# Hybrid encoder layer on one core: the first half's second norm through ones matmuls, its output projection ahead of the second half's mixers, the sample's modulation loads in one buffer

## The chip, the core and the metric

The kernel runs on one core of a Trainium2 chip. The core has TensorE (PE in the rows; PEld is its weight load), VectorE (DVE), ScalarE (ACT), GpSimd (POOL) and SyncE (SP), each with a queue that it works off in order, and 16 DMA engines. Times are device microseconds (us) of one execution; the metric is the median of three runs.

## What is computed

One layer of a streaming encoder over two groups of frames that share the weights: a prompt of 1024 frames and a sample of 64, of 1024 channels each. Around the code that the change touches, the reference is:

```python
mod = (silu(c) @ w_ada + b_ada).reshape(B, 6, 1, D_MODEL)     # one set for the prompt, one for the sample
h = rms_norm(x, norm_mix) * (1 + scale1) + shift1
u = h @ w_in                                                  # split into conv, delta, pool, attention
mix = concat([conv, gated_delta, pool, stick_breaking]) @ w_out
x = x + gate1 * mix
h2 = rms_norm(x, norm_ffn) * (1 + scale2) + shift2            # the second norm
x = x + gate2 * ((silu(h2 @ w_gate) * (h2 @ w_up)) @ w_down)
```

`rms_norm` is `x * rsqrt(mean(x * x) + eps) * g` over the 1024 channels. The gated delta mixer solves a lower triangular system in each chunk of 64 frames and carries a state from chunk to chunk.

## The kernel before

Channels lie on the 128 partitions, eight tiles deep, and frames along the free dimension. The frames are worked in two halves: HA, the first 512 of the prompt, and HB, the other 512 and the 64 of the sample (576 columns). Every large product is made of three passes, weight-high by x-high, weight-high by x-low and weight-low by x-high: `load_w` loads a weight tile (wraw, 512 KB, from SyncE's queue), ScalarE copies its high part (whi) and VectorE subtracts for the low part (wlo), each with two buffers. `gemm_fm` then runs the matmuls into a bank that `gemm_bank` gives. Up to the sixth pair of the FFN's tiles that is one of two banks; from there (`wide`) it takes turns over eight, some of which the delta mixer and the attention also use, by a counter `turn` that every call moves on.

The order of the code at the end of the kernel is: projection and mixers of HA (`mixers`: `delta`, `sb_attn`, and for HA `conv` and `pool`), projection of HB, mixers of HB with the sample's attention, output projection and second norm of HA (`out_proj`), FFN of HA (`ffn`, which calls `conv` and `pool` of HB on its way), then `out_proj` and `ffn` of HB. A scheduler lays the instructions out per engine by that order as priority, by what is ready, and with `tc.high_priority()` for what others wait for; so on each engine HA's FFN and HB's mixers interleave. An engine then keeps to its list.

- The delta mixer solves its systems in blocks. VectorE writes nl, SyncE sends it to memory (nld), GpSimd brings it back transposed, does the substitution of the smallest blocks (fst, fsu) and writes X; `pw<-cst,X` on TensorE is the first matmul that needs it. HB has three such blocks, the third with the sample.
- The second norm of a half: after each output tile m, `residual` adds it to x (xA in HA, VectorE), `sumsq` squares it (sq, ScalarE) and adds it to acc (VectorE). Then `rstd_of` sums acc over the partitions by a product with a matrix of ones (pn, in fp32, two instructions of TensorE), and ScalarE takes Ln and Exp. `modulate` writes nrm (VectorE), its high part hi (ScalarE) and its low part lo (VectorE), from which the FFN's first pg starts.
- The modulation of the sample: `ada_sample` loads 32 tiles wads of 512 KB with SyncE, behind a weight's load in its queue, and VectorE multiplies and sums each. Their buffers are the tiles k2 and q2 of the attention. They are shared out over the tiles of HA's FFN from tile t0_s on. The prompt's loads are named wadt. The tile raw holds the delta mixer's inputs, and at the end parts of HB's mixed output.

## Time and profile before

| | us |
|---|---|
| median of three runs | 1483.85 |
| lowest, highest | 1481.14, 1489.55 |
| the profiled execution | 1479.19 |
| its span | 1477.4 |
| TensorE busy in it | 1396.9 |
| VectorE busy | 1025.3 |
| ScalarE busy | 662.5 |

The span is the time between the first and the last instruction; all times of rows count from its start. The mean clock granted to TensorE over the span is 0.976 of full speed, where 1.00 stands for 2.4 GHz and 0.5 for 1.2 GHz. In a timeline row a number in brackets is the idle time just before the instruction, with what ended it; several instructions in one row are marked xN. Ends of matmuls are modelled, so the starts of neighbours tell better what one takes.

### The profile page before, as it was taken

What the parts mean: (1) busy time and instruction counts of PE and PEld (TensorE: products, weight loads), DVE (VectorE), ACT (ScalarE), POOL (GpSimd) and SP (SyncE); (2) the same over time, 40 slices, a digit from 0 to 9 for tenths busy, and PEclk for the clock granted to TensorE, in tenths of its full rate; (3) what the DMA queues carried; (4) which work ended last, traced back from release to release, by engine and by line L of the source; (5) the groups of instructions that cost most, each with busy time, mean ns of one, the idle gap of its engine ahead of it and who ended that gap; (6) DMA issues with size and microseconds to landing.
All of it is one profiled execution on the core that took longest, in us unless ns stands there. A gap on an engine that the chain in (4) does not pass through costs nothing.

```text
span 1477.4 us, 24764 instructions
## 1 busy us (share of the span) xinstructions
PE 1396.9 (95%) x9824; PEld 1219.4 (83%) x9824; DVE 1025.3 (69%) x1816; ACT 662.5 (45%) x1191; POOL 119.8 (8%) x246
## 2 busy tenths in 40 slices
PE   8999999979997799799999899999899999999998
PEld 5777898868875477587877688889799999999998
DVE  8788997954898998846766677764755455554444
ACT  4467555744664478447766332222522222222221
POOL 0005000500014000500140000000000000000000
PEclk9999999989998799999999999999999999999999
DMA  8776655555845223424324566542322222222222
GB/s 319 246 221 183 194 169 177 172 166 164 266 141 160 70 90 96 124 76 134 111 75 133 164 226 209 196 140 86 127 77 84 86 86 86 77 82 86 87 86 93
DMA packets 98547, 205.43 MB, mean 139 GB/s; under 512 B 30848, under 2 KB 40928, under 8 KB 98432
## 3 DMA queue, kind: packets, MB, share of 16 engines
q1 hardware_dynamic: 89888, 191.68, 38.8%
q0 software_dynamic: 8544, 12.17, 3.8%
q8 instruction: 77, 1.26, 0.3%
q14 instruction: 38, 0.31, 0.1%
HBM read 175.57 MB, written 28.24 MB: 138 GB/s over the span
## 4 chain that ended last, share of the span: by engine, by line
PE 73%; DVE 14%; DMA 6%; ACT 3%; issue 3%; SPq 0%; POOL 0%; DVEq 0%; ACTq 0%
PE pg L138 61%; DVE cy L126 2%; DMA wadt<-in_wadat_dram 2%; PE psC L141 2%; PE pk L138 2%; DVE wlo L123 2%; DMA X<-xd 1%; PE psO L141 1%; PE z L141 1%; DVE dnf L126 1%; PE pw L138 1%; DVE wadt L212 1%; DVE lo L126 1%; ACT whi L117 1%; DVE xA L126 1%
## 5 line engine op out<-in xcount | busy, mean ns | idle before, releaser
L138 PE MATMUL pg<-hi,whi 128*128 128x288 f32 (+1 forms) x1504 | 503.7, 336 | 9.9 <-DVE sbo L123 2.7
L138 PE MATMUL pg<-hi,wlo 128*128 128x288 f32 (+1 forms) x1504 | 498.7, 332 | 3.4 <-DVE wlo L123 3.4
L138 PE MATMUL pg<-lo,whi 128*128 128x288 f32 (+1 forms) x1504 | 498.0, 331 | 1.6 <-DVE lo L126 1.6
L117 ACT ACTIVATE whi<-wraw 128x1024 fp32r<-128x1024 f32 (+2 forms) x192 | 199.7, 1041 | 474.0 <-PE pg L138 414.4
L138 PEld LDWEIGHTS pg<-hi,whi 128*128 128x128 f32 x1504 | 285.4, 190 | 41.4 <-issue 9.2
L138 PEld LDWEIGHTS pg<-hi,wlo 128*128 128x128 f32 x1504 | 285.1, 190 | 28.3 <-DVE wlo L123 4.7
L138 PEld LDWEIGHTS pg<-lo,whi 128*128 128x128 f32 x1504 | 285.7, 190 | 25.5 <-issue 2.1
L123 DVE TENSOR_TENSOR wlo<-wraw,whi 128x1024 fp32r<-128x1024 f32 (+2 forms) x192 | 230.4, 1201 | 106.2 <-ACT whi L117 103.5
L138 PE MATMUL pg<-g,whi 128*128 128x288 f32 (+1 forms) x1056 | 251.4, 330 | 4.1 <-DVE xA L126 1.9
L138 PEld LDWEIGHTS pg<-g,whi 128*128 128x128 f32 x1056 | 177.5, 188 | 20.2 <-DVE xA L126 3.2
L138 PE MATMUL pg<-g,wlo 128*128 128x288 f32 (+1 forms) x528 | 171.4, 328 | 0.0
L126 DVE SCALAR_TENSOR_TENSOR xs<-pg,mod,xs 128x288 f32<-128x288 f32 (+2 forms) x288 | 106.4, 412 | 85.8 <-PE pg L138 84.6
L123 DVE TENSOR_TENSOR fa<-fa,pg 128x288 f32<-128x288 f32 (+1 forms) x66 | 35.0, 531 | 101.5 <-PE pg L138 98.3
L138 PEld LDWEIGHTS pg<-g,wlo 128*128 128x128 f32 x528 | 99.2, 188 | 7.5
L126 DVE SCALAR_TENSOR_TENSOR cy<-cvb,vec,cy 128x512 f32<-128x512 f32 (+1 forms) x120 | 93.4, 792 | 0.2
L126 DVE SCALAR_TENSOR_TENSOR xA<-pg,mod,xA 128x512 f32<-128x512 f32 x96 | 69.6, 745 | 13.0 <-PE pg L138 12.6
L114 ACT ACTIVATE e<-e 128x512 f32<-128x512 f32 (+4 forms) x100 | 52.1, 521 | 0.9
L138 PE MATMUL pg<-mixs,whi 128*128 128x288 f32 x256 | 50.8, 295 | 0.0
L212 DVE CUSTOM_DVE_ANT_0 wadt<-wadt,cb,vec 128x1024 f32<-128x1024 f32 x32 | 40.9, 1280 | 12.2 <-DMA wadt<-in_wadat_dram 12.1
L114 ACT ACTIVATE zs<-zs 128x512 f32<-128x512 f32 (+4 forms) x50 | 25.8, 516 | 45.8 <-DVE zs L123 43.6
L212 DVE CUSTOM_DVE_ANT_0 wads<-wads,cb,vec 128x1024 f32<-128x1024 f32 x32 | 41.0, 1280 | 5.1 <-DMA wads<-in_wadat_dram 5.0
L138 PEld LDWEIGHTS pg<-mixs,whi 128*128 128x128 f32 x256 | 41.0, 188 | 0.1
(299 smaller groups left out, 1842.3 us busy)
## 6 DMA issues: line engine op xcount, KB each, us to landing
wraw<-in_wgate_dram SPq DMA_DIRECT2D x44, 512.0 KB, 3.2
wraw<-in_wup_dram SPq DMA_DIRECT2D x44, 512.0 KB, 3.3
wraw<-in_wdown_dram SPq DMA_DIRECT2D x44, 512.0 KB, 3.2
wadt<-in_wadat_dram SPq DMA_DIRECT2D x32, 512.0 KB, 4.7
wads<-in_wadat_dram SPq DMA_DIRECT2D x32, 512.0 KB, 4.4
wraw<-in_wfm_dram SPq DMA_DIRECT2D x30, 512.0 KB, 3.7
wraw<-in_wout_dram SPq DMA_DIRECT2D x16, 512.0 KB, 3.5
xA<-in_xa_dram SPq DMA_DIRECT2D x16, 256.0 KB, 5.4
```

Source lines behind the costliest of these rows:

```text
L114: nc.scalar.activation(out, in_, func, bias=bias, scale=scale)
L117: nc.scalar.activation(out, in_, ACTF.Copy)
L123: nc.vector.tensor_tensor(out=out, in0=a, in1=b, op=op)
L126: nc.vector.scalar_tensor_tensor(out, a, s, b, op0, op1)
L138: return nc.tensor.matmul(out, lhsT=lhsT, rhs=rhs, start=start, stop=stop)
L141: nc.tensor.matmul(out, lhsT=lhsT, rhs=rhs, start=start, stop=stop, skip_group_check=True)
L212: nc.vector.tensor_tensor_reduce(out=junk, in0=w, in1=cbt[g], scale=1.0, scalar=V("b_ada", col), op0=ALU.mult, op1=ALU.add, accum_out=mod[ ...
```

## The change

HA's second norm no longer adds squares on VectorE: each m's squares go to TensorE as they come, as one of eight products with the matrix of ones that accumulate in one bank, taken from the pool "cv" and not by `gemm_bank`. HB's second norm stays. `rstd_of` and `modulate` take the finished sum. The tiles wads lie in the delta mixer's raw tile, of which there is one, and start at tile 8 of the FFN in place of 12. The call of HA's output projection and the last loads of the prompt's modulation stand ahead of HB's mixers.

```diff
--- before.py
+++ after.py
@@ -252,7 +252,7 @@
 
     def ada_sample(j0, j1):
         for j in range(j0, j1):
-            t = sb.tile([P, 1024], F32, tag=("k2", "q2")[j % 2], name="wads")
+            t = dn.tile([P, 1560], F32, tag="raw", name="wads")[:, 0:1024]
             with behind():
                 nc.sync.dma_start(out=t, in_=io["wadat"][j])
             ada_dve(t, 16 + j, (1,))
@@ -264,9 +264,9 @@
         tt(s2[:, :, g], s2[:, :, g], V("norm_ffn"), ALU.mult)
 
 
-    def rstd_of(h, acc, early):
-        pns = []
-        for c0, n in h.chunks:
+    def rstd_of(h, acc, early, summed=None):
+        pns = [] if summed is None else [(summed, 0, h.n)]
+        for c0, n in h.chunks if summed is None else []:
             pn = (PD if pns else PC)("pn") if early else gemm_bank("pn")
             mm(pn[:, 0:n], C("ones"), acc[:, c0:c0 + n])
             pns.append((pn, c0, n))
@@ -305,8 +305,8 @@
             act_(h.hi[k][:, c], t[:, c], ACTF.Identity, bias=sh)
             stt(h.lo[k][:, c], t[:, c], sh, f(h.hi[k][:, c]), ALU.add, ALU.subtract)
 
-    def modulate(h, acc, sc, shift0, in_place=False):
-        r = rstd_of(h, acc, in_place)
+    def modulate(h, acc, sc, shift0, in_place=False, summed=None):
+        r = rstd_of(h, acc, in_place, summed)
         h.hi, h.lo = [], []
         for k in range(KT):
             modulate_k(h, k, r, sc, shift0, in_place)
@@ -1049,14 +1049,20 @@
                 split(h, t, hi[k], lo[k])
             load_x(h, h.samp)
         acc = new_acc()
+        pn = None if h.samp else PC("pn")
         for m in range(KT):
             for ps, c0, n in gemm_fm(h, io["wout"][m], hi, lo, order):
                 with tc.high_priority():
                     residual(h, m, 16, ps, c0, n)
             with tc.high_priority():
-                sumsq(h, acc, m)
+                if h.samp:
+                    sumsq(h, acc, m)
+                else:
+                    q = ST("sq")
+                    act_(q[:, 0:h.n], h.xt[m][:, 0:h.n], ACTF.Square)
+                    mm(pn[:, 0:h.n], C("ones"), q[:, 0:h.n], m == 0, m == KT - 1)
         with tc.high_priority():
-            modulate(h, acc, s2, 24)
+            modulate(h, acc, s2, 24, summed=pn)
 
     def ffn(h):
         if h.samp and DEFER:
@@ -1103,7 +1109,7 @@
                 if c == FT // FCH - 1:
                     nc.sync.dma_start(out=h.y[:, m], in_=h.xt[m][:, 0:n_])
 
-        t0_s = 12
+        t0_s = 8
         a = gate(0)
         for c in range(FT // FCH):
             if not h.samp and c == 1:
@@ -1178,11 +1184,11 @@
     while len(ada_left) > 8:
         ada_step()
     scale2(0)
-    mixers(HB)
     out_proj(HA)
     with tc.high_priority():
         while ada_left:
             ada_step()
+    mixers(HB)
     ffn(HA)
     out_proj(HB)
     ffn(HB)
```

What the scheduler makes of it shows in three places. The numbers in names (pw_4582) count buffers and differ between the two programs.

On TensorE, in HB's second delta block near 490 us, before:

```order
L141 MATMUL z<-q_5591,k_5589 128x512 x2
L138 MATMUL py<-W,X 64x64 x16
L138 MATMUL px<-X,W 64x64 x16
L141 MATMUL psC<-sh,omu_r 128x512
L141 MATMUL psC<-sl,omu_r 128x512
L141 MATMUL psO<-ph,v_5590 128x512
L141 MATMUL psC<-sh,u_r 128x512
L138 MATMUL pw<-Y,nl 64x64 x16
L141 MATMUL psO<-pl,v_5590 128x512
L138 MATMUL pn<-acc,cst 128x512
L141 MATMUL psC<-sl,u_r 128x512
```

and with the change:

```order
L138 MATMUL pw<-Y,nl 64x64 x5
L141 MATMUL psC<-sl,u_r 128x512
L141 MATMUL z<-q_6011,k_6009 128x512 x2
L138 MATMUL pn<-sq,cst 128x512
L138 MATMUL py<-W,X 64x64 x13
L138 MATMUL pn<-sq,cst 128x512
L138 MATMUL py<-W,X 64x64 x3
L138 MATMUL px<-X,W 64x64 x16
L141 MATMUL psC<-sh,omu_r 128x512
L141 MATMUL psC<-sl,omu_r 128x512
```

Here py and px belong to the triangular solve and psC, psO and z to the attention. The norm's sum is complete ahead of the last py of a solving step, where one pn of acc stood behind the next step's pw. Six more pn<-sq stand further up, five of them ahead of the block's first pw<-cst,X.

On TensorE, ahead of the first matmul of HB's third delta block (near 627 us in the trace of before), before:

```order
L138 MATMUL pg<-g_7466,whi 128x512 x2
L138 MATMUL pg<-g_7466,wlo 128x512
L138 MATMUL pg<-g_7541,whi 128x512 x2
L138 MATMUL pg<-g_7541,wlo 128x512
L138 MATMUL pw_5063<-cst,X 64x64
L141 MATMUL psO<-pl,v_5815 128x512
L141 MATMUL psC<-sl,u_r 128x128
L138 MATMUL pw_5063<-cst,X 64x64 x15
L141 MATMUL z<-q_6041,k_6039 128x384 x2
```

and with the change:

```order
L138 MATMUL pg<-hi_4703,whi 128x512
L138 MATMUL pg<-lo_4704,whi 128x512
L138 MATMUL pg<-hi_4703,wlo 128x512
L138 MATMUL pg<-hi_4709,whi 128x512
L141 MATMUL psO<-pl,v_6460 128x128
L138 MATMUL pw_5483<-cst,X 64x64
L138 MATMUL pg<-lo_4710,whi 128x512
L138 MATMUL pg<-hi_4709,wlo 128x512
L138 MATMUL pg<-hi_4715,whi 128x512
L138 MATMUL pw_5483<-cst,X 64x64 x15
```

pg<-g is the second product of the FFN's pair of tiles, pg<-hi the first of the next tile. The first pw<-cst,X of the block stood behind the last pg<-g; now it stands in the next tile's products, with 31 instructions more between it and the second block's.

On SyncE's queue, where HA's FFN loads its weights and HB's last delta block begins, before:

```order
L323 DMA wraw<-in_wdown_dram 128x1024 x2
L865 DMA out_dn_p_dram<-S_p 128x128
L323 DMA wraw<-in_wup_dram 128x1024
L323 DMA wraw<-in_wgate_dram 128x1024
L853 DMA mixB<-kbe 128x2x256
L626 DMA gate<-udnB 128x2x64
L491 DMA mixB<-sbo 64x512
L176 DMA xs<-in_xb_dram 128x576
L323 DMA wraw<-in_wup_dram 128x1024
L777 DMA nld_124<-nl 64x128 x2
```

and with the change:

```order
L323 DMA wraw<-in_wdown_dram 128x1024 x2
L257 DMA wads<-in_wadat_dram 128x1024 x2
L865 DMA out_dn_p_dram<-S_p 128x128
L323 DMA wraw<-in_wup_dram 128x1024
L491 DMA mixB<-sbo 64x512
L323 DMA wraw<-in_wgate_dram 128x1024
L257 DMA wads<-in_wadat_dram 128x1024
L853 DMA mixB<-kbe 128x2x256
L626 DMA gate<-udnB 128x2x64
L257 DMA wads<-in_wadat_dram 128x1024
L323 DMA wraw<-in_wup_dram 128x1024
L176 DMA xs<-in_xb_dram 128x576
```

Four loads wads now stand among these weights, each behind the one before in the only buffer; in the program before the first stands 14 rows further down than the last row here.

## Rows read from the trace of the kernel before

**Rows 1.** The page: busy time by engine, and the chain that ended last.
```profile
PE 1396.9 (95%) x9824; PEld 1219.4 (83%) x9824; DVE 1025.3 (69%) x1816; ACT 662.5 (45%) x1191; POOL 119.8 (8%) x246
...
PE 73%; DVE 14%; DMA 6%; ACT 3%; issue 3%; SPq 0%; POOL 0%; DVEq 0%; ACTq 0%
...
L117 ACT ACTIVATE whi<-wraw 128x1024 fp32r<-128x1024 f32 (+2 forms) x192 | 199.7, 1041 | 474.0 <-PE pg L138 414.4
```

**Rows 2.** Stretches of 40 us: busy time and instructions by engine, clock, DMA.
```profile
core 0: us, PE busy (x) PEld busy (x) DVE busy (x) ACT busy (x) POOL busy (x), PEclk, DMA share, GB/s
440.00:480.00 40.00, 30.18 (x226) 23.34 (x225) 35.65 (x57) 18.56 (x31) 19.46 (x37) 0.87 0.50 152
480.00:520.00 40.00, 29.15 (x224) 20.68 (x220) 39.23 (x62) 17.73 (x37) 0.66 (x2) 0.79 0.25 66
520.00:560.00 40.00, 38.75 (x260) 30.54 (x260) 38.43 (x63) 29.91 (x57) 1.09 (x2) 1.00 0.30 94
560.00:600.00 40.00, 40.00 (x303) 31.07 (x301) 36.27 (x64) 29.87 (x52) 4.25 (x8) 1.00 0.45 126
600.00:640.00 40.00, 29.57 (x168) 21.77 (x168) 27.64 (x53) 19.44 (x47) 18.68 (x39) 0.91 0.30 94
800.00:840.00 40.00, 33.22 (x143) 24.74 (x142) 27.04 (x44) 16.67 (x31) 0.00 (x0) 0.91 0.50 160
840.00:880.00 40.00, 40.00 (x176) 32.70 (x175) 28.82 (x39) 16.37 (x21) 0.00 (x0) 1.00 0.59 208
```

**Rows 3.** Timeline of TensorE: start, us, engine, line, operation, idle before.
```profile
397.03 1.03 PE L138 MATMUL pl<-dne,cst 128*128 128x512 f32 x2
...
466.52 0.44 PE L138 MATMUL pw<-cst,X 64*64 64x64 f32 x2 [8.60 <-DMA X<-xd]
...
486.30 0.80 PE L141 MATMUL psO<-pl,v 128*128 128x512 f32 x1 [1.26 <-DVE pl L123]
486.90 2.07 PE L138 MATMUL pn<-acc,cst 128*128 128x512 f32 x2
```

**Rows 4.** Timeline of VectorE from the last xA of HA to nrm.
```profile
477.43 0.75 DVE L126 SCALAR_TENSOR_TENSOR xA<-pg,mod,xA 128x512 f32<-128x512 f32 x1 [1.28 <-PE pg L138]
...
486.16 0.68 DVE L123 TENSOR_TENSOR acc<-acc,sq 128x512 f32<-128x512 f32 x1
...
495.47 2.73 DVE L126 SCALAR_TENSOR_TENSOR nrm<-xA,s,acc 128x512 f32<-128x512 f32 x4
```

**Rows 5.** Timelines of VectorE and TensorE around the third block.
```profile
587.39 0.68 DVE L126 SCALAR_TENSOR_TENSOR nl<-pkk,W 128x512 f32<-128x512 f32 x1
...
627.11 0.44 PE L138 MATMUL pw<-cst,X 64*64 64x64 f32 x2 [6.06 <-DMA X<-xd]
...
632.17 0.39 PE L138 MATMUL pg<-hi,whi 128*128 128x512 f32 x1
632.40 0.40 PE L138 MATMUL pg<-lo,whi 128*128 128x512 f32 x1
```

**Rows 6.** The instructions that write or read wads, and the page on wlo.
```profile
L257 SPq DMA_DIRECT2D wads<-in_wadat_dram x32: 327/328/526, 808.3 to 965.5; - x32
L212 DVE CUSTOM_DVE_ANT_0 wads<-wads,cb,vec x32: 1273/1280/1289, 812.1 to 970.1; 128x1024 f32<-128x1024 f32 x32
  DMA wads<-in_wadat_dram: 5.0, 9
...
DMA to landing us min/median/max: 3.4/4.4/6.5
...
L123 DVE TENSOR_TENSOR wlo<-wraw,whi 128x1024 fp32r<-128x1024 f32 (+2 forms) x192 | 230.4, 1201 | 106.2 <-ACT whi L117 103.5
```

**Rows 7.** Timelines of VectorE and TensorE near the end of the sample's attention.
```profile
826.38 1.22 DVE L123 TENSOR_TENSOR wlo<-wraw,whi 128x1024 fp32r<-128x1024 f32 x1
...
827.66 0.79 PE L138 MATMUL pg<-hi,wlo 128*128 128x512 f32 x1 [2.03 <-DVE wlo L123]
...
838.17 0.47 PE L138 MATMUL pg<-hi,whi 128*128 128x512 f32 x1 [2.65 <-DVE sbo L123]
```

## The prediction

> **What bounds the kernel now.** I read the page first: TensorE is busy 95% of the span and VectorE 69%, and the chain that ended last is 73% TensorE [rows 1]. An average over stages hides where the other 5% lies, so the second view is the table by stretches of 40 us [rows 2]. It shows three kinds of stretch. From 440 to 520 VectorE is nearly full (35.65 and 39.23 of 40) while TensorE is busy 30.18 and 29.15 and its granted clock is 0.87 and 0.79: here HA's output projection, its second norm, its first FFN matmuls and HB's delta mixer meet, and VectorE decides. From 600 to 640 both have holes. From 640 on TensorE is nearly full, as 840 to 880 shows, except for 800 to 840 (33.22, clock 0.91). So a microsecond of VectorE is worth something only before 640, and a microsecond of TensorE work after that is worth a microsecond.
>
> The third view, the timeline around the long waits, names what ends them. TensorE sits 8.60 us before HB's second delta block and 6.06 us before the third, both for the DMA X<-xd [rows 3, 5]. The second wait follows a chain that nothing shortens: VectorE writes nl at 587.39, SyncE sends it, GpSimd transposes, substitutes and sends X, and TensorE starts at 627.11 [rows 5]: 39.7 us from nl to the matmul. HA's second norm begins when the last residual xA ends at about 478.1, its sum goes to TensorE as pn at 486.90, and the first nrm, from which the FFN starts, is written at 495.47 [rows 3, 4].
>
> **The change, part by part.**
>
> *Squares on TensorE.* Seven additions acc<-acc,sq go, about 0.6 us of VectorE each (0.68 with the tail that overlaps the next) [rows 4], 4.2 us in all. Four of them lie before the 8.60 us wait, whose chain started ahead of the first of them, so these give nothing there. The last three, 1.8 us, lie where VectorE decides. On TensorE one pn of two instructions goes and eight come. Such a matmul took 1.03 us at the full clock (pl<-dne) and 2.07 us at the half clock (pn) [rows 3], so eight cost 8.2 us and the net is about +7.2. In the new order five of the eight stand ahead of the matmul that waits 8.60 us: 5.2 us, hidden by that wait. One follows it and two stand among the py, where TensorE waits for VectorE anyhow: the wait of 1.26 us in [rows 3] is one of this stretch. I cost all eight at nothing; without that cover they would cost up to 7.2.
>
> *The order.* With HA's projection ahead of HB's mixers in the code, the instructions up to about 424 us stay where they were, and after that HA's norm and FFN stand ahead of pieces of HB's mixers. On VectorE 10.0 us of work then stand between the start of the last xA (477.43) and the first nrm, which so comes at about 487.4 in place of 495.47, and the FFN starts some 7 us sooner. That alone is no gain: the wait at 627 follows nl, and nl must be early for it. In the new order, with the durations of the rows of before, VectorE has 2.1 us more to do up to nl than it had. Its idle time from 440 to 600 is 4.35, 0.77, 1.57 and 3.73 us [rows 2], 10.4 in all, so nl moves between +2.1 (no idle filled) and -8.3 (all filled). Most of that idle time is for matmuls and DMAs that stay, so I take a value near the upper end, **-2.0**, and keep both. On SyncE's queue nl's two DMAs now stand behind the loads of two weights and a write of mixB that they stood ahead of; what these wait for (wlo of the weight before, the pool's plm) stands ahead of nl on VectorE and ScalarE too, so they add nothing unless that order is upset. Two more table loads on ScalarE fall near 850, where it is busy 16.37 of 40 us [rows 2], and cost nothing.
>
> *Work ahead of the wait.* Between the first matmul pw<-cst,X of the second block (466.52) and that of the third (627.11), TensorE has 743 instructions in place of 712: 31 more, at 0.232 us each (starts 632.17 and 632.40 [rows 5]) 7.2 us. From there to the sample's attention near 816 it has 29 fewer and 5.4 us less by the same rates. TensorE came to the wait at 621.05; with 7.2 more it comes at 628.3, less what the earlier FFN start fills of the 10.85 us of idle time between 480 and 520 [rows 2]. I take 5 of these, so it comes at 623.3, and X at 625.1: the wait shrinks from 6.06 to about 2. Since TensorE is full afterwards, the smaller rest comes off the end: **-5.4**.
>
> *The clock.* A mean of 0.91 over 600 to 640 is 7.2 us at 1.2 GHz in place of 2.4, so 3.6 us of work lost; they follow the 6.06 us wait, as after the one of 2.03 us, where a matmul of 512 columns takes 0.79 us (827.66 [rows 7]) and not 0.39 (632.17 [rows 5]). With a wait of 2 us there may be none of it, or all: between 0 and -3.6, I take the middle, **-1.8**.
>
> *The sample's modulation loads.* 32 loads wads of 512 KB, each read once by VectorE for 1.28 us, start in before at 808 because their two buffers are held by attention [rows 6]. Two of them stand in front of wlo at 826.38, for which TensorE waits 2.03 us; a further 2.65 us is for sbo, which holds the bank of the next pg [rows 7]. Idle time of 6.8 us and a clock of 0.91 cost about 10 us in this stretch [rows 2]. In the new order the loads start about 705 and twelve (before: six) are read before the sample's attention ends, so wlo comes sooner. The eight banks of the wide mode shift by one, as the norm takes none, so that another pg meets the bank that sbo frees. So the 2.03 goes and the 2.65 stays: **-2.0**, with ends of 0 (a new wait takes its place) and -6.
>
> *One buffer for them.* A load can start only when VectorE has read the one before: 1.28 + 0.33 for the issue + 4.4 to land is 6.0 us a round [rows 6], against 24 matmuls of 0.232 or 5.57 us for a weight. Where the order has one load for each weight, VectorE loses 0.4 us each time. A weight is split as soon as the one two before it is done, so 5.57 less 1.04 (whi) and 1.20 (wlo) [rows 1, 6], 3.3 us, are spare. I take **+1.0**, from 0 to 3. This is where a rule speaks against the change. The Trainium skill, page "Trainium Kernel Development and Optimization", section Best Practices, asks for double buffers so that DMA and compute overlap. By it each load would show its whole landing time on VectorE, 31 times 4.4 us. In the trace, with two buffers, VectorE waited for these loads 5.0 us in all, in nine cases; no run here yet shows one buffer.
>
> The sum is -2.0 - 5.4 - 1.8 - 2.0 + 1.0 = -10.2 us. On the profiled execution, 1479.19 us, that gives 1469.0. The median of the three runs of before, 1483.85, is 4.66 us above that execution, so I forecast **1473.7 us**, 0.7% less; the rivals' times are on that median too.
>
> **The rivals.** *The wait stays what it is.* nl comes 2.1 us later, TensorE still waits and falls to the half clock, and the bank takes the place of wlo at 827. Then 2.1 - 5.4 + 0 + 0 + 1.0 = -2.3, or 1481.6. For it speaks that the 39.7 us behind nl are fixed and that VectorE has more to do before it; against it that VectorE had up to 10 us idle on the way. That the swap of the code lines does nothing by itself (no instruction moves before 424 us) belongs here too.
>
> *The early start carries through.* nl 6 us earlier, no half clock, both waits near 830 gone: -6 - 5.4 - 3.6 - 3 + 1 = -17, or 1466.8. For it speaks that the FFN is there 7 us sooner to fill holes; against it that VectorE is at 39.23 of 40 in the very stretch.
>
> *Slower: the one buffer holds up the weights.* VectorE is in order, so a wads that waits keeps the wlo behind it, and SyncE's queue keeps the wraw loads behind a wads that waits for its buffer. If a load takes 4.8 us to land (3.4 to 6.5 were seen [rows 6]), a round is 6.4, 0.84 over a weight, and 31 rounds that TensorE waits for are +26: -11.2 + 26 is +14.8, or 1498.7. It decides from about 0.6 us a round, if the loads stand back to back. Against it: they are spread over some 270 us, 8.7 us each. By the Trainium skill's rule above it would come out so.
>
> **How the numbers follow.** I give the forecast 0.42, the unchanged wait 0.29, the carry-through 0.15, the slower case 0.14. A measurement of this kernel can tell about 0.5%, 7.4 us, from no change. Of the forecast's case 0.37 lie beyond that bound, with the carry-through 0.52 for faster; 0.05 and the unchanged wait make 0.34 for the same; 0.14 for slower. The range reaches from 1465, with the carry-through in it, to 1487, above the unchanged wait and a little of the slower case.
>
> **What would show it.** Right: no acc<-acc,sq of 512 columns after 424 us, nrm near 488, nl between 579 and 590, a wait before the third block's pw<-cst,X under 4 us, a clock over 0.91 in its stretch, no wait for wlo near 827, and waits for wads of a few microseconds in all. Wrong: nl after 592, TensorE waiting for wlo or whi between 705 and 975 several times, or more TensorE idle time before 500 than before because pn waits for sq.

## The result, and the profile after

The changed kernel takes 1497.9 us (median of five runs, 1495.58 to 1499.35) against 1483.85 before (five runs, 1481.14 to 1489.55). The ratio is 1.0081, with a 95% interval of 1.0055 to 1.0108: slower, where I had forecast 0.7% less. The profiled execution is the one of 1497.9 us, its span 1496.1.

The page after, busy time by engine and the chain that ended last, to be held against [rows 1]:

```profile
PE 1413.6 (94%) x9838; PEld 1229.0 (82%) x9838; DVE 1022.8 (68%) x1809; ACT 663.3 (44%) x1193; POOL 119.9 (8%) x246
...
PE 64%; DVE 17%; DMA 9%; issue 4%; POOL 3%; ACT 2%; SPq 1%; DVEq 0%; ACTq 0%; POOLq 0%
```

TensorE has 14 instructions more than in [rows 1] and is busy 16.7 us longer, VectorE 2.5 us less. My price for the added products was 7.2 us net. Of the 16.7 us, 5.3 lie before the 45th weight (the marks are explained below), where both kernels have the same instructions, so they belong to the executions and not to the change. 9.9 lie between the 70th and the 98th weight, where the granted clock is 0.956 in place of 0.984. The table by stretches shows where (columns as in [rows 2]):

```profile
core 0: us, PE busy (x) PEld busy (x) DVE busy (x) ACT busy (x) POOL busy (x), PEclk, DMA share, GB/s
440.00:480.00 40.00, 35.15 (x208) 26.61 (x207) 37.97 (x60) 19.11 (x31) 20.95 (x40) 0.96 0.45 136
480.00:520.00 40.00, 33.22 (x306) 23.98 (x304) 37.47 (x57) 19.00 (x33) 2.26 (x4) 0.91 0.34 91
...
600.00:640.00 40.00, 31.86 (x211) 24.71 (x210) 30.37 (x64) 18.90 (x45) 19.56 (x42) 0.91 0.27 75
...
760.00:800.00 40.00, 31.36 (x155) 23.82 (x154) 22.76 (x38) 17.65 (x30) 5.17 (x9) 0.87 0.45 107
800.00:840.00 40.00, 39.52 (x219) 30.45 (x218) 27.30 (x45) 19.88 (x39) 0.76 (x1) 1.00 0.45 142
840.00:880.00 40.00, 31.25 (x121) 24.21 (x120) 19.19 (x27) 16.48 (x24) 0.00 (x0) 0.89 0.53 164
```

From 440 to 520 TensorE is busier than in [rows 2] (68.4 us against 59.3) at a clock of 0.96 and 0.91 where it had 0.87 and 0.79. From 760 to 880 stand two new holes, with a clock of 0.87 and 0.89; there [rows 2] had one, from 800 to 840.

To set two executions side by side I use the weights: the start of the k-th whi on ScalarE, counted from 0. Up to the 45th, near 400 us, all kernels have the same instructions, yet their profiled executions reach it between 399.9 and 409.5 us, so I compare from there on. In the changed kernel the way from the 45th to the 70th weight (663.6 us) takes 257.1 us in place of 265.0, so 7.9 less. From the 70th to the 78th it takes 70.1 for 66.0, from the 78th to the 92nd 120.0 for 113.7, from the 92nd to the 98th 43.1 for 32.1, and from there to the end 599.3 for 600.4.

These marks lie on ScalarE, and the new order moves TensorE's work across them. TensorE begins 1650 instructions from the 45th to the 70th weight where before has 1697, and 500 for 439 from there to the 78th. So the 7.9 us are not a gain by themselves. Taken together, 45 to 78 has 2150 instructions for 2136 (the norm's 14) and takes 327.2 us for 331.0, so 3.8 us were gained. From 78 to 98 both have 681, and the change takes 163.1 us for 145.8: here 17.3 us were lost.

TensorE's timeline in the first of the two regions, the second delta block, the end of the norm and the third delta block:

```profile
471.26 0.29 PE L138 MATMUL pw<-cst,X 64*64 64x64 f32 x2 [4.45 <-DMA X<-xd]
...
483.71 1.02 PE L138 MATMUL pn<-sq,cst 128*128 128x512 f32 x2
...
490.20 0.50 PE L141 MATMUL psO<-pl,v 128*128 128x512 f32 x1 [1.26 <-DVE pl L123]
...
624.63 0.38 PE L141 MATMUL psC<-sh,u_r 128*128 128x256 f32 x1 [1.68 <-ACT sh L117]
627.76 0.45 PE L141 MATMUL psO<-ph,v 128*128 128x128 f32 x1 [2.75 <-DMA v<-svB]
...
634.61 0.33 PE L138 MATMUL pw<-cst,X 64*64 64x64 f32 x2
```

The wait ahead of the second block has shrunk from the 8.60 us of [rows 3] to 4.45; five of the norm's products stand ahead of it. The first pw<-cst,X of the third block has no bracket any more; the 6.06 us of [rows 5] are gone, and waits of 1.68 and 2.75 us for the attention stand ahead of it. And the second region, every TensorE wait over 0.5 us between 762 and 880:

```profile
767.60 0.29 PE L138 MATMUL pw<-cst,X 64*64 64x64 f32 x2 [3.27 <-DMA X<-xd]
...
785.03 0.27 PE L141 MATMUL z<-q2s,k2s 128*128 128x64 f32 x1 [4.13 <-DMA q2s<-sqB]
786.55 0.39 PE L141 MATMUL z<-q2s,k2s 128*128 128x64 f32 x1 [1.25 <-DMA q2s<-sqB]
...
843.80 0.50 PE L138 MATMUL pg<-hi,whi 128*128 128x512 f32 x1 [0.91 <-ACT whi L117]
845.07 0.50 PE L138 MATMUL pg<-hi,wlo 128*128 128x512 f32 x1 [0.53 <-DVE wlo L123]
854.62 0.77 PE L138 MATMUL pg<-hi,whi 128*128 128x512 f32 x1 [4.17 <-DVE sbo L123]
875.32 1.22 PE L138 MATMUL pg<-g,whi 128*128 128x512 f32 x2 [3.14 <-DVE fa L123]
```

These are 17.4 us of waiting, and both stretches around the longer ones ran at a mean clock under 0.9 (0.87 and 0.89). Of the two waits of [rows 7] the one of 2.03 us for wlo is gone, and the one for sbo has grown from 2.65 to 4.17. The other four long ones are new and belong to two chains.

*The sample's delta block.* The X at 767.60 is that of a fourth, small block, the sample's own, which my prediction did not look at. VectorE's timeline ahead of it, with the first and the last of four reads of wads:

```profile
708.98 1.28 DVE L212 CUSTOM_DVE_ANT_0 wads<-wads,cb,vec 128x1024 f32<-128x1024 f32 x1 [1.23 <-DMA wads<-in_wadat_dram]
...
730.20 1.28 DVE L212 CUSTOM_DVE_ANT_0 wads<-wads,cb,vec 128x1024 f32<-128x1024 f32 x1
...
734.45 0.28 DVE L126 SCALAR_TENSOR_TENSOR nl<-pkk,W 128x128 f32<-128x128 f32 x1
```

The four are read ahead of that block's nl. In the kernels below that have norm and swap too but later loads nl comes 1.9 us before the 78th weight (2.8 in before), here 0.8 us after it. And the chain's own small transfers, xd and X, now run beside loads wads of 512 KB on top of those of the weights. The DMA view of the changed kernel from 757 to 770 us (last column: median us from issue to landing):

```profile
wads<-in_wadat_dram SPq DMA_DIRECT2D x1, 512.0 KB, 4.2
xd<-fst POOLq DMA_DIRECT2D x4, 4.0 KB, 3.2
X<-xd POOLq DMA_DIRECT2D x2, 32.0 KB, 4.0
```

and the same view, from 753 to 765 us, of a kernel below (e11_no_wads_bank) whose loads wads start after the block:

```profile
xd<-fst POOLq DMA_DIRECT2D x4, 4.0 KB, 1.9
X<-xd POOLq DMA_DIRECT2D x2, 32.0 KB, 2.1
```

*The gate beside the loads.* The 3.14 us at 875.32 are for fa<-fa,pg, which reads tile 13's up product out of its bank. ScalarE's timeline:

```profile
868.23 1.28 ACT L114 ACT_TABLE_LOAD   x1
869.52 0.60 ACT L114 ACTIVATE fa<-pg 128x512 f32<-128x512 f32 x1
870.14 1.28 ACT L114 ACT_TABLE_LOAD   x1
871.43 0.63 ACT L114 ACTIVATE fe<-fe 128x512 f32<-128x512 f32 x1
...
875.30 0.63 ACT L117 ACTIVATE g<-fa 128x512 fp32r<-128x512 f32 x1 [2.66 <-DVE fa L123]
```

and VectorE's:

```profile
866.85 1.28 DVE L212 CUSTOM_DVE_ANT_0 wads<-wads,cb,vec 128x1024 f32<-128x1024 f32 x1 [2.24 <-DMA wads<-in_wadat_dram]
...
868.06 0.68 DVE L126 SCALAR_TENSOR_TENSOR fe<-fa,fe 128x512 f32<-128x512 f32 x1
...
872.10 0.69 DVE L123 TENSOR_TENSOR fa<-fa,fe 128x512 f32<-128x512 f32 x1 [2.22 <-ACT fe L114]
...
873.38 1.28 DVE L212 CUSTOM_DVE_ANT_0 wads<-wads,cb,vec 128x1024 f32<-128x1024 f32 x1
...
874.58 0.68 DVE L123 TENSOR_TENSOR fa<-fa,pg 128x512 f32<-128x512 f32 x1
```

The sigmoid of tile 13 (fe) goes back and forth between the two engines. From tile 14 on (`SILU_T`) ScalarE computes the gate at once with another table; its fa<-pg now stands between two steps of tile 13's sigmoid, which makes two table loads more. VectorE's fe at 868.06 stood behind a wads that waited 2.24 us, and another wads stands between the two steps of fa. The g made of this fa is only begun at 875.30, 0.02 us ahead of TensorE's pg<-g, and finished later; so TensorE did not wait for that data but, by these rows, for the bank that fa set free.

### The profile page after: what moved, and what is told of

Its sections match the earlier page's. It is cut to its first block, busy times and chain, and to the rows that moved or that the text cites. A ratio compares the mean times of both kernels' runs of the same rounds, so it can differ in the third digit from the quotient of the medians.

```text
span 1496.1 us, 24777 instructions
## 1 busy us (share of the span) xinstructions
PE 1413.6 (94%) x9838; PEld 1229.0 (82%) x9838; DVE 1022.8 (68%) x1809; ACT 663.3 (44%) x1193; POOL 119.9 (8%) x246
## 4 chain that ended last, share of the span: by engine, by line
PE 64%; DVE 17%; DMA 9%; issue 4%; POOL 3%; ACT 2%; SPq 1%; DVEq 0%; ACTq 0%; POOLq 0%
PE pg L138 56%; DVE wlo L123 2%; DVE cy L126 2%; DMA wadt<-in_wadat_dram 2%; PE psC L141 1%; DVE lo L126 1%; DVE xA L126 1%; DVE dnf L126 1%; DMA X<-xd 1%; DVE junk L212 1%; POOL fst L135 1%; PE z L141 1%; DVE wadt L212 1%; PE pw L138 1%; POOL fsu L135 1%
## 5 line engine op out<-in xcount | busy, mean ns | idle before, releaser
L138 PE MATMUL pg<-g,whi 128*128 128x288 f32 (+1 forms) x1056 | 256.5, 335 | 6.3 <-DVE fa L123 3.1
L126 DVE SCALAR_TENSOR_TENSOR xs<-pg,mod,xs 128x288 f32<-128x288 f32 (+2 forms) x288 | 106.5, 412 | 85.7 <-PE pg L138 83.9
L212 DVE CUSTOM_DVE_ANT_0 wads<-wads,cb,vec 128x1024 f32<-128x1024 f32 x32 | 41.0, 1282 | 18.2 <-DMA wads<-in_wadat_dram 17.8
```

The costliest lines, as they stand in the source:

```text
L126: nc.vector.scalar_tensor_tensor(out, a, s, b, op0, op1)
L138: return nc.tensor.matmul(out, lhsT=lhsT, rhs=rhs, start=start, stop=stop)
L212: nc.vector.tensor_tensor_reduce(out=junk, in0=w, in1=cbt[g], scale=1.0, scalar=V("b_ada", col), op0=ALU.mult, op1=ALU.add, accum_out=mod[ ...
```

## The experiments

All ratios are to the kernel before on the same chip, with 95% intervals. The five columns of stages are read from each profiled execution as above: us from the 45th weight to the 70th, the 78th, the 92nd, the 98th and the end.

| kernel | median us | ratio | 45-70 | 70-78 | 78-92 | 92-98 | 98-end |
|---|---|---|---|---|---|---|---|
| before | 1483.85 | 1 | 265.0 | 66.0 | 113.7 | 32.1 | 600.4 |
| the change | 1497.9 | 1.0081 [1.0055, 1.0108] | 257.1 | 70.1 | 120.0 | 43.1 | 599.3 |
| after_again | 1498.87 | 1.0089 [1.0058, 1.012] | 256.6 | 71.2 | 117.8 | 42.1 | 599.3 |
| e1_wads_only | 1486.26 | 0.999 [0.9967, 1.0013] | 268.8 | 68.0 | 107.3 | 33.2 | 600.4 |
| e3_norm_only | 1489.23 | 1.0019 [1.0, 1.0039] | 271.6 | 63.3 | 115.9 | 35.6 | 599.3 |
| e4_swap_only | 1478.49 | 0.9944 [0.9912, 0.9977] | 272.0 | 63.0 | 103.4 | 33.2 | 600.3 |
| e4_again | 1476.69 | 0.995 [0.9933, 0.9968] | 271.2 | 63.0 | 103.2 | 33.2 | 600.3 |
| e2_no_wads | 1483.59 | 0.9979 [0.9958, 1.0] | 257.2 | 69.7 | 110.4 | 36.8 | 599.3 |
| e5_raw_late | 1496.59 | 1.0077 [1.0049, 1.0105] | 262.9 | 69.2 | 111.7 | 40.7 | 605.8 |
| e7_two_early | 1498.06 | 1.0086 [1.0062, 1.011] | 256.8 | 68.6 | 117.3 | 50.7 | 599.3 |
| e9_swap_wads | 1483.47 | 0.998 [0.9954, 1.0006] | 270.8 | 65.6 | 106.2 | 33.2 | 600.3 |
| e14_silu_16 | 1492.59 | 1.0047 [1.0018, 1.0077] | 259.1 | 70.9 | 118.8 | 41.1 | 599.3 |
| e6_bank_kept | 1488.78 | 1.0043 [1.0017, 1.0068] | 258.0 | 71.1 | 117.2 | 32.8 | 600.6 |
| e11_no_wads_bank | 1482.36 | 0.9961 [0.9935, 0.9986] | 256.8 | 68.9 | 113.4 | 32.1 | 600.5 |
| e12_raw_late_bank | 1488.16 | 1.0013 [0.9987, 1.0039] | 263.1 | 68.9 | 116.6 | 33.2 | 608.6 |
| e15_bank_only | 1491.11 | 1.006 [1.0036, 1.0083] | 260.8 | 66.0 | 107.9 | 48.2 | 599.4 |
| e13_raw_ten_bank | 1486.6 | 1.0015 [0.9993, 1.0036] | 260.0 | 69.0 | 121.8 | 33.2 | 600.3 |
| e10_norm_wads | 1491.94 | 1.0072 [1.0049, 1.0095] | 271.6 | 63.0 | 115.0 | 36.5 | 599.4 |
| e17_norm_bank | 1480.53 | 0.9967 [0.9947, 0.9987] | 269.4 | 63.3 | 105.6 | 31.7 | 601.1 |
| e18_two_early_bank | 1488.52 | 1.0016 [0.9991, 1.0042] | 257.4 | 68.5 | 121.0 | 30.6 | 600.4 |

The change's own row has the medians of the result; the other kernels have their own runs of before, with medians from 1482.98 to 1488.19 us.

A stage is read from one execution, so small differences in it say little. Eleven of these kernels (all with norm and swap) have the same instruction lists up to the 74th weight, and from the 45th to the 70th they take from 256.6 to 263.1 us. The three with neither (before, e1, e15) take 265.0, 268.8 and 260.8. The stages also hold different work where the order differs: with the swap alone TensorE begins 1765 instructions from 45 to 70 where before has 1697. I therefore go by the ratios first, and by stages where two kernels have the same lists up to the stage.

### Each part alone

My first theory was that the loads in one buffer are the loss and the other parts gain. Its rival was that the norm's products cost.

The loads alone, on the kernel before:

```diff
-            t = sb.tile([P, 1024], F32, tag=("k2", "q2")[j % 2], name="wads")
+            t = dn.tile([P, 1560], F32, tag="raw", name="wads")[:, 0:1024]
...
-        t0_s = 12
+        t0_s = 8
```

> The kernel before with the loads alone changed: wads in the delta mixer's one raw tile, from FFN tile 8; norm and order as before. Theory A (the one buffer: in the changed kernel VectorE waited 17.8 us for wads in place of 5.0, and the time from 760 to 880 us grew by some 17 us): it is slower than before by 10 to 18 us, so 1494 to 1502, and VectorE waits over 12 us for wads. Theory B (the new order: the sample's attention stands nearer to its loads, the third mixer block's wait and the bank of sbo fall badly): within 4 us of before, 1480 to 1488, with the waits for wads hidden. Theory C (half each): about 1491.

Measured 0.999, theory B. In the order of before one buffer and an early place in the code cost nothing that can be told.

The norm alone (all of the diff on `rstd_of`, `modulate` and `out_proj`, the rest as before):

```diff
+        pn = None if h.samp else PC("pn")
...
-                sumsq(h, acc, m)
...
+                    mm(pn[:, 0:h.n], C("ones"), q[:, 0:h.n], m == 0, m == KT - 1)
```

> The kernel before with the second norm's squares of HA on TensorE alone; loads and order of the code as before. Theory A: no loss, 1476 to 1485, the norm's first nrm some 5 us or more sooner. Theory B, if the order that the norm brings is the cause and not the swap of the calls: 1490 or more. If the eight matmuls are not hidden: +7, so 1491, with TensorE's idle time no less than before.

Measured 1.0019, or 1489.23 us, between the two theories. The swap of the calls alone, twice:

```diff
-    mixers(HB)
     out_proj(HA)
     with tc.high_priority():
         while ada_left:
             ada_step()
+    mixers(HB)
```

> The kernel before with HA's output projection and the last loads of the prompt's modulation ahead of HB's mixers, nothing else. Theory A: within 5 us of before, 1479 to 1489. Theory B, if the swap is what upsets the order: 1490 or more, with a long wait for q2s or sbo as in the changed kernel.

> The kernel before with the swap of the calls alone, once more, with more rounds. If its gain is one of the place of instructions, it is there again: 4 to 11 us under before, ratio 0.993 to 0.997. If it was a chance of those runs: 0.998 to 1.001.

Measured 0.9944 and, with more rounds, 0.995: a gain that holds, that neither theory of the first run had, and the lowest ratios of all, though the intervals of the next best (e11, e17) overlap theirs. The sample's delta block is through earlier, so z<-q2s starts 26.8 and 26.7 us after the 78th weight (50.6 in before), and neither wait of [rows 7] is left. The stage from 78 to 92 is 10 us shorter, but 45 to 70 is 6 to 7 us longer, as part of the work has moved there; 5 to 6 us are left. The third part undone, so norm and swap together:

```diff
-            t = dn.tile([P, 1560], F32, tag="raw", name="wads")[:, 0:1024]
+            t = sb.tile([P, 1024], F32, tag=("k2", "q2")[j % 2], name="wads")
...
-        t0_s = 8
+        t0_s = 12
```

> The changed kernel with the loads put back: wads in k2 and q2, from FFN tile 12; norm on TensorE and new order stay. Theory A: the loss of 760 to 880 us goes and the gain of some 4 us up to 700 us stays: 1476 to 1484. Theory B: the loss stays, 1492 to 1499, with TensorE waiting about 4 us for q2s near 785 and 4 us for sbo near 855. Theory C: about 1488.

Measured 0.9979, theory A: without the change of the loads the loss goes. And the changed kernel once more, unedited:

> The changed kernel once more, beside the next three. Both theories: 0.5 to 1.1% slower than before. It tells how far the four long waits of TensorE between 760 and 880 us (3.3 for X, 4.1 and 1.3 for q2s, 4.2 for sbo, 3.1 for fa, each with a stretch at 1.2 GHz behind it) belong to the kernel and not to one execution: if they do, the new trace has them within 1 us each.

Measured 1.0089. The waits are there again: 3.14 us for fa and 3.19 for sbo as expected, but 2.22 for X and 2.51 and 1.06 for q2s, so two of them fell by more than the 1 us that I had allowed. So parts of 0.999, 1.0019 and 0.995 make 1.008 together. The loss is no sum; it lies in what the parts do to each other.

### The loads, and two of their features apart

On the changed kernel, the late start in one buffer, then two buffers with the early start:

```diff
-        t0_s = 8
+        t0_s = 12
```

> The changed kernel with the loads wads still in the one raw tile, but shared out from FFN tile 12 as before. Theory D (it is the early loads, which stand in VectorE's and SyncE's lists ahead of the sample's delta block and attention, that make X, q2s and fa late): the waits for X and q2s near 765 and 785 shrink under 2 us, and it is 0.3 to 0.8% faster than the changed kernel, 1485 to 1494. Theory E (one buffer is enough to lose it, wherever the loads start): no faster than the changed kernel, and VectorE waits over 15 us for wads.

```diff
-            t = dn.tile([P, 1560], F32, tag="raw", name="wads")[:, 0:1024]
+            t = sb.tile([P, 1024], F32, tag=("k2", "q2")[j % 2], name="wads")
```

> The changed kernel with the loads in k2 and q2 again, two buffers, but shared out from FFN tile 8. They can't start before the attention gives k2 and q2 back, so what is early in the code is late on the queue, and the loads crowd behind it. Theory D: as fast as without the change of the loads, 1480 to 1489, as no load stands ahead of the sample's delta block. Theory E: the same. If the crowd of loads costs by itself: over 1490, with TensorE waiting for wlo between 800 and 880.

Measured 1.0077 and 1.0086, both like the change: theory E for the first, and for the second the crowd of loads, with TensorE waiting 4.25 and 1.54 us for wlo. Undoing one of the two features removes nothing; only both together (e2) do. So beside norm and swap either feature is enough for the loss. e5 loses 6.5 us after the 98th weight, where it is late: its raw tile is still in use when HB's mixed output needs it, as e12's TensorE timeline shows too (the same loads, below):

```profile
997.75 0.61 PE L138 MATMUL pg<-mixs,whi 128*128 128x288 f32 x1 [3.47 <-DVE mixs L123]
```

e7 loses 18.6 us between the 92nd and the 98th. Then the swap with the loads, without the norm (e4 and the edit of e1):

```diff
-    mixers(HB)
     out_proj(HA)
...
+    mixers(HB)
...
-        t0_s = 12
+        t0_s = 8
```

> The kernel before with the swap of the calls and the loads in the one raw tile from tile 8, but the norm as before (its bank too). The swap alone was 0.994, the loads alone 0.999. If it is the early loads in the new order that cost (nl of the sample's delta block later by its reads of wads on VectorE, then X and q2s): 3 to 8 us slower than the swap alone, 0.997 to 1.000. If the loss needs the norm on TensorE and its bank: as the swap alone, 0.993 to 0.996.

Measured 0.998: the loads may cost some 0.3% on the swap (the interval overlaps that of the swap alone), but 92 to 98 stays at 33.2 us. Among the kernels so far that stage was long in all that had the norm and short in all that had not. That points to the banks: the norm no longer calls `gemm_bank`, and so shifts the counter `turn` by one for every later product.

### The bank counter

The changed kernel with the one call given back to the counter:

```diff
         pn = None if h.samp else PC("pn")
+        turn[0] += 0 if h.samp else 1
```

> The changed kernel with the counter of the banks moved on by one where HA's norm used to take a bank, so that the eight banks of the wide mode fall on the same products as before. Theory F (the shifted bank meets the attention's bank later): the wait of 4.2 us for sbo near 855 falls under 2.7 and it is 4 to 7 us faster than the changed kernel. Theories D and E: within 3 us of it, as the other three long waits stay.

Measured 1.0043, theory F. The stage from 92 to 98 is 32.8 us, and the hole near 860 is gone; what is left is the delta block's part (X still waits 2.2 us, z 4.5). The same line in e2 and in e5:

```diff
-        t0_s = 8
+        t0_s = 12
+        turn[0] += 0 if h.samp else 1
```

> Norm on TensorE and the new order, loads as before (k2 and q2, from tile 12), and the counter of the banks moved on by one as HA's norm used to move it. Theory F (the shifted bank is a loss of its own between the 84th and 98th weight: another product meets the attention's bank, and ScalarE loads its tables twice more): 3 to 5 us faster than the same kernel with the shifted bank (ratio 0.998), so 0.994 to 0.996 of before, with one table load there in place of three. Theory G (the bank costs only where the loads crowd): 0.997 to 0.999 as without it.

> The changed kernel with the loads in the one raw tile from tile 12 and the counter of the banks moved on by one. With the shifted bank this was 1.0077 of before, with no long wait for X, and 8.6 us lost between the 92nd and 98th weight. Theory F: that loss goes, 1.000 to 1.003. Theory G or the one buffer by itself: still 1.005 or more, VectorE waiting over 20 us for wads.

Measured 0.9961 and 1.0013, where the shifted ones had 0.9979 and 1.0077; the first pair can't be told apart, the second can by its ratios. Its profiled executions don't show where: from the 45th weight to the end e5 and e12 take the same 1090.2 and 1090.4 us. Next the table loads by themselves. With the change of the gate's table two tiles later, the changed kernel has one table load between 850 and 910 in place of three:

```diff
-SILU_T = 14
+SILU_T = 16
```

> The changed kernel with the tile from which HA's FFN takes its gate by the Silu table put from 14 to 16; all else as in the changed kernel. If the two extra table loads, which stand in the chain of the gate of tile 13, make the wait of 3.1 us for fa near 873 and the half clock behind it: that wait goes and it is 4 to 7 us faster than the changed kernel, 1.004 to 1.006 of before. If the wait is made by the loads wads on VectorE's list: within 2 us of the changed kernel, 1.007 to 1.010.

Measured 1.0047. The wait for fa falls from 3.14 to 0.66 us, but a wait of 1.90 for wlo comes at 885, and the stage still takes 41.1. The ratio lies where the first theory has it, but its interval overlaps that of the change, and 78 to 98 takes 159.9 us as in the change's repeat (163.1 in the change). e5 also has one table load there, and 40.7 us. So what the two table loads cost in the changed kernel isn't shown; they are not all that the shift brings. Last the shift with nothing else, on the kernel before:

```diff
         with tc.high_priority():
             modulate(h, acc, s2, 24)
+            turn[0] -= 0 if h.samp else 1
```

> The kernel before with one edit: the counter of the eight banks steps back by one behind HA's second norm, so that every later product of the wide mode gets the bank that it has in the changed kernel. Norm, order of the calls and loads are those of before. In its order ScalarE has 9 table loads where before has 5. Theory A (the shift costs by itself: another product meets the attention's bank, and the gates and sigmoids of two tiles mix on ScalarE): 2 to 8 us over before, ratio 1.001 to 1.005, and 35 to 38 us from the 92nd to the 98th weight where before has 32.1. Theory B (the shift costs only where the modulation's loads crowd VectorE at that place, that is with loads from tile 8 on): no loss, ratio 0.998 to 1.001, and 32 to 34 us for these six weights.

Measured 1.006, with the stage at 48.2 us: theory A's direction, beyond its bands. That stage alone overstates it: it is 16.1 us longer than in before, but 78 to 98 together only 10.3. So one step of a counter costs 0.6% with no norm, no swap and two buffers. TensorE's timeline of this run:

```profile
860.53 0.73 PE L138 MATMUL pg<-g,whi 128*128 128x512 f32 x2 [1.35 <-ACT fa L114]
...
869.45 1.22 PE L138 MATMUL pg<-g,whi 128*128 128x512 f32 x2 [7.96 <-DVE fa L123]
```

and ScalarE's:

```profile
858.58 1.28 ACT L114 ACT_TABLE_LOAD   x1
...
861.07 1.28 ACT L114 ACT_TABLE_LOAD   x1
862.36 0.63 ACT L114 ACTIVATE fe<-fe 128x512 f32<-128x512 f32 x1
863.01 1.28 ACT L114 ACT_TABLE_LOAD   x1
...
864.95 1.28 ACT L114 ACT_TABLE_LOAD   x1
866.24 0.63 ACT L114 ACTIVATE fe<-fe 128x512 f32<-128x512 f32 x1
```

ScalarE loads four tables in 7.7 us, one for nearly each step of tile 13's sigmoid, and VectorE's fa waits for the last of them; TensorE waits 7.96 us for the bank, as it does in e7 with the same four loads. The one table load that before has there stands at 857.50 ahead of the gate of tile 14, behind the whole sigmoid.

What the norm does without the shift is seen by itself (e3 and the counter's line):

```diff
         pn = None if h.samp else PC("pn")
+        turn[0] += 0 if h.samp else 1
```

> The kernel before with the norm's sum on TensorE and the bank counter kept as in before; order of the calls and loads as in before. Theory A (the shift of the banks was the loss in the norm alone, which ran at 1.002 with it; the norm itself gains by its earlier nrm and costs nothing on TensorE): 3 to 9 us under before, ratio 0.994 to 0.998, and 32 to 34 us from the 92nd to the 98th weight. Theory B (the eight products cost what the shorter chain gives): ratio 0.999 to 1.002.

Measured 0.9967, theory A, against 1.0019 with the shift; the eight products cost less than the shorter chain gives. With the shift (e3) TensorE waits in that region for the splits of two weights, with one table load and not three:

```profile
838.79 0.79 PE L138 MATMUL pg<-hi,whi 128*128 128x512 f32 x1 [3.13 <-ACT whi L117]
...
876.81 0.79 PE L138 MATMUL pg<-hi,wlo 128*128 128x512 f32 x1 [3.40 <-DVE wlo L123]
```

Without it (e17) TensorE has no wait over 1.8 us from 760 to 900, and its stretch there (columns as above) is full where the changed kernel had 31.25:

```profile
840.00:880.00 40.00, 40.00 (x176) 32.72 (x175) 28.50 (x39) 16.09 (x20) 0.00 (x0) 1.00 0.66 224
```

The six pairs with and without the shift can be set side by side more sharply than by the stages. Each pair has the same list on TensorE up to its 5550th matmul, near 820 us, and on the other engines up to about there. From the start of that matmul to the end of the execution the traces give, in us:

| pair | shifted | kept | difference |
|---|---|---|---|
| e15 and before | 667.7 | 659.3 | 8.4 |
| the change (its repeat) and e6 | 667.1 (665.1) | 656.8 | 10.3 (8.3) |
| e3 and e17 | 665.4 | 657.3 | 8.1 |
| e7 and e18 | 678.1 | 666.1 | 12.0 |
| e5 and e12 | 673.0 | 670.1 | 2.9 |
| e2 and e11 | 660.6 | 660.0 | 0.6 |

So in four of the six the shift costs 8 to 12 us behind the place where the lists part. In the two whose loads start late beside norm and swap it costs little there.

### Which pairs are enough, and one buffer by itself

Norm and loads without the swap (e3 and the edit of e1):

```diff
-        t0_s = 12
+        t0_s = 8
...
+        pn = None if h.samp else PC("pn")
```

> The kernel before with the norm on TensorE (and so the shifted bank) and the loads in the raw tile from tile 8 on, without the change of the order of the calls. Theory A (the loss needs all three, since the new order of the calls is what puts the early loads ahead of the sample's delta block on VectorE): 0 to 5 us over before, ratio 1.000 to 1.003. Theory B (bank and early loads together are enough): 7 us or more over before, ratio over 1.005, with 40 us or more from the 92nd to the 98th weight.

Measured 1.0072, theory B by the ratio, though not by its stage: 92 to 98 takes 36.5 us, not 40. By the ratio the swap is not needed for a loss of this size. The profiled execution does not show where the loads cost: from the 78th weight to the end it takes 750.9 us, e3's without the change of the loads 750.8. Then the loads of the changed kernel from tile 10 on, with the counter kept, to start neither before the sample's delta block nor too late:

```diff
-        t0_s = 8
+        t0_s = 10
...
+        turn[0] += 0 if h.samp else 1
```

> The changed kernel with the bank counter kept as in before and the loads from tile 10 on in place of tile 8, in the raw tile. Theory A (the loads from tile 8 on cost because they stand ahead of the sample's delta block, those from tile 12 on because the one tile is in use until HB's mixed output needs it): tile 10 has neither, so 3 to 8 us under before as without the loads in one buffer, ratio 0.994 to 0.998, and no wait over 1 us for X near 765 nor for the mixed output near 998. Theory B (one buffer costs by itself, wherever the loads start): between the run from tile 8 on and the one from tile 12 on, 1.001 to 1.004.

Measured 1.0015, in theory B's band; theory A wanted 0.994 to 0.998 and fell. nl is as early as without loads (1.9 us before the 78th weight), no wait for mixs is left, and yet X is late by a wait of 2.93 us. Its DMA view from 750 to 762 us says why:

```profile
wads<-in_wadat_dram SPq DMA_DIRECT2D x2, 512.0 KB, 4.2
...
xd<-fst POOLq DMA_DIRECT2D x4, 4.0 KB, 3.5
X<-xd POOLq DMA_DIRECT2D x2, 32.0 KB, 2.7
```

One of the two loads, issued at 750.87, is under way until 754.92. The block's four xd are issued from 751.21 on; the first three land right behind it, at 755.10 to 755.47, and the fourth at 756.67, beside a weight's load that is issued at 753.22. They take 3.5 us (median) in place of 1.9, and from nl to the last X pass 34.1 us where e11 has 30.8. So the collision of the transfers delays X even where VectorE's order doesn't. Last, two buffers with the early place in the code and the counter kept (e7 and the line):

```diff
-            t = dn.tile([P, 1560], F32, tag="raw", name="wads")[:, 0:1024]
+            t = sb.tile([P, 1024], F32, tag=("k2", "q2")[j % 2], name="wads")
...
+        turn[0] += 0 if h.samp else 1
```

> The changed kernel with the bank counter kept and the loads in the two tiles of the attention, in the code from tile 8 on (they are held up to about 800 there). Theory A (without the shift the crowd of the loads behind 800 costs little, and no load runs beside the sample's delta block): ratio 0.996 to 1.000, 32 to 36 us from the 92nd to the 98th weight, where the same kernel with the shift had 50.8. Theory B (the crowd of the loads on VectorE is the loss, whichever bank the products get): ratio over 1.004 and 40 us or more.

Measured 1.0016, slightly over theory A's band; 92 to 98 takes 30.6 us where e7 had 50.7. Its loss lies from 78 to 92 (121.0), where the loads that were held up come close together, and TensorE waits for the wlo behind them:

```profile
PE pg L138 <- DVE wlo L123: 5.3, 2, 2.9
```

With the counter kept, four kernels now stand in a square: two buffers from tile 12 have 0.9961 (e11), one buffer from tile 12 has 1.0013 (e12), two from tile 8 have 1.0016 (e18) and one from tile 8 has 1.0043 (e6). By these ratios either feature costs about half a per cent and both 0.8%, though the intervals of the last three overlap. The traces bear out the price of the late one buffer only in part: e12's execution is 6.3 us slower than e11's, and e5's 5.7 slower than e2's, already from the 45th to the 70th weight, with the same instructions and before any load wads; why isn't known. Not tried: smaller early loads, which would price the collision alone, and a second raw tile.

## Why the prediction was wrong

**What came as told.** nrm is written at 492.18, so 85.7 us after the 45th weight (95.3 in before, from [rows 4]): 9.6 us sooner, I said 8. The eight products of the norm cost less than they give (e17), and the second block's wait took up those ahead of it. The wait for X of the third block went from 6.06 us to nothing; I had left 2.

**What came by less, or not as told.** My terms for the order, the work and the clock were -2.0 - 5.4 - 1.8 = -9.2. Norm and swap without the two losses below (e11) run at 0.9961, so 5.8 us faster; the interval reaches from 2.1 to 9.6 us, and -9.2 is just inside it. But nl came 190.3 us after the 45th weight and not earlier than before's 187.2, so +3.1 where I took -2.0, past my upper end of +2.1; and the clock from 600 to 640 stayed at 0.91, as waits of 1.68 and 2.75 us stand where the old one stood. The third block's first pw came 228.1 us after the 45th weight (227.0 in before), with 43 more of TensorE's instructions ahead of it. From there to the 78th weight TensorE has 29 fewer, 789 for 818, and the way takes 99.1 us in place of 104.0: 4.9 less, where I had 5.4. So the gain is the work ahead of the wait, and not an earlier nl.

VectorE's timeline of the changed kernel for the two:

```profile
492.18 2.73 DVE L126 SCALAR_TENSOR_TENSOR nrm<-xA,s,acc 128x512 f32<-128x512 f32 x4
...
596.77 0.68 DVE L126 SCALAR_TENSOR_TENSOR nl<-pkk,W 128x512 f32<-128x512 f32 x1
```

**The step that failed first** is the one on the banks, in the prediction's part on the sample's loads: "another pg meets the bank that sbo frees" and "So the 2.03 goes and the 2.65 stays". The 2.03 did go, and the 2.65 became 4.17. But I priced the shift as one wait at one bank. It gave every later product of the wide mode another bank, and the engines' lists differ from about 820 us on. The shift alone costs 0.6% (e15), 0.5% with the norm (e3 against e17), 0.4% in the full change (e6 against the change, two intervals that overlap; 10.3 and 8.3 us behind the common mark), and 0.7% in e7 against e18. Between e2 and e11 it can't be told from nothing. What TensorE then waits for is not one thing: sbo and fa in the change, fa behind four table loads in e15, whi and wlo in e3.

With it goes the sentence that two more table loads near 850 "cost nothing". I had held them against ScalarE's busy share, 16.37 of 40 us, which tells nothing of a chain that goes back and forth between two engines. In e15 TensorE waits 7.96 us for the end of such a chain with four loads in it. In the changed kernel, without the two loads, the wait of 3.14 us falls to 0.66 but others come (e14), so their price there stays open.

**The second** is the price of the loads: -2.0 for their earlier start, and +1.0, with an upper end of 3, for one buffer. Norm and swap with the counter kept run at 0.9961 without the loads' change (e11) and at 1.0043 with it (e6): 0.8%, or 12 us lost. Both terms fail, as the early place alone costs 0.5% (e18 against e11) and so does the one buffer alone (e12 against e11). I gave the loads 3.3 us of slack for each weight, which was right for wlo: behind the 98th weight the loads go on to 989 us, and 599.3 us to the end are no more than before. But other things stand behind the loads too. On VectorE it is the nl of the sample's block, on the DMA engines xd and X, which no queue shows as a neighbour, and between 800 and 850 the wlo (e18) and sbo. I had looked at the first three blocks and not at the fourth, since before it waits 0.66 us only. Of the 12 us I can place the late X and z (the stages from 70 to 92 together are 6.0 us longer in e6 than in e11); the rest is not placed. With the one buffer from tile 12 on, 6 to 8 us lie behind the 98th weight (605.8 and 608.6 us to the end in e5 and e12, 599.3 and 600.5 in e2 and e11), where HB's mixed output wants the tile.

**The rival that came nearest** gave 1498.7 us for one buffer that holds up the weights, and the time was 1497.9, but its mechanism is not the one. It had 31 rounds of 0.84 us each; VectorE waited for these loads 17.8 us in 16 cases, half the loads, and the weights after 900 us were never late. The view of the tile (us in all, times):

```profile
  DMA wads<-in_wadat_dram: 17.8, 16
```

The Trainium skill, page "Trainium Kernel Development and Optimization", section Best Practices, asks for double buffers to overlap DMA with compute. The runs agree where the loads start late: two buffers have 0.9979 and 0.9961 (e2, e11), one has 1.0077 and 1.0013 (e5, e12), though much of that is the tile that HB's mixed output wants and not the landing. With the early place they don't tell: 1.0086 with two (e7) against 1.0081 and 1.0089 with one, and with the counter kept 1.0016 (e18) against 1.0043 (e6), two intervals that overlap. There the two buffers are held by the attention up to about 800, so that e7 and e18 start their loads late as well.

**The swap that does nothing by itself**, as I wrote in the first rival, is wrong as well: alone it has the lowest ratio (0.9944 and 0.995). The norm alone gains too (0.9967), and the two together have 0.9961, so the gains don't add. Why they don't isn't shown.

**Open** is why the loads cost nothing in the order of before (e1, 0.999) and 0.8% with norm and swap, beyond what X and z explain. For the late X itself the traces give both parts: in the change nl comes 2.7 us later against the 78th weight than in e11 (VectorE's order), and from nl to the last X pass 33.2 us in place of 30.8 (the chain with its transfers); e13 has the second part alone, 34.1 us. What a later X is worth in the ratio no run here shows by itself. Open too is why the shift costs so little behind the common mark in e2 and e5.

## What to carry to other kernels

A call that is taken out of a rotation by counter moves every later user of that rotation; give the count back, or look at the places where the rotation meets a buffer that is held long. Stages between two marks on one engine can be compared only if they hold the same work: count the instructions of the engine that matters. A load that is moved ahead has to be held against every list that it passes, on the engine that reads it and on the DMA engines, up to the next chain of small dependent steps, and not against its own consumer alone. And parts that measured -0.1, +0.2 and -0.5% alone made +0.8% together, so a change of three parts is measured with each part left out.

## What the runs showed of the hardware

- **Small transfers beside large ones.** Four xd of 4 KB from GpSimd's queue landed in 1.9 us (median) in e11, where no 512 KB load was under way ahead of them, and in 3.2 and 3.5 us behind one (the change, e13). Two X of 32 KB took 2.1 us in e11, with a weight's load under way for most of it, and 4.0 and 2.7 with a load wads beside them as well. A weight's load does it too: in before the fourth xd, issued 0.2 us behind a wraw, took 3.18 us and landed 0.2 us after it. I had counted the loads against SyncE's queue alone. The Trainium skill, page "DMA: Bandwidth & Descriptors", section Issuing engines are not separate DMA queues, says that transfers issued by different engines run on the same 16 DMA engines and interleave. The rows agree, as a transfer of GpSimd's was late behind one of SyncE's; here a chain of two dependent transfers paid at both steps.
- **A table load in a chain.** Each of the 114 in the twenty traces took 1.283 us. The Trainium skill, page "ScalarE activation tables: per-element evaluation and per-set limits", section What a function is on this engine, gives 1283 ns between functions of different sets; the trace agrees. What surprised me is that a bank on TensorE's side can change how many there are: between 850 and 910 us 1 in before, 3 with the change, and 5 with the shift alone, four of them in a row. It does not always: e3, e5 and e10 have the shift and 1.
- **The same instructions, 10 us apart.** Up to the 45th weight the kernels have one and the same program, and their profiled executions reach it between 399.9 and 409.5 us. Comparisons of two profiled executions by their absolute times are good to that only. From a common mark on, a stage differs by under 1 us between e4 and its repeat and by 2.2 us between the change and its repeat, but by 8.0 us, from the 45th to the 70th weight, among before, e1 and e15, whose instructions are the same there. The wait for X at the third block is 6.06, 5.99 and 2.33 us in these three.
